# One expert-weight unit per branch, nine raw buffers, and a reordered start, in a two-layer hybrid trunk

## Chip, cores and metric

One core of one Trainium2 chip runs the whole program. The metric is device time in microseconds (us), the median of three runs. Engine names are those of the profile: PE (matrix products), DVE, ACT, POOL (element-wise work), SP (here it only issues loads).

## What is computed

A two-layer trunk on 256 tokens of 1024 columns, all in float32. Each layer has a token mixer and a feed-forward part; each part is normed, modulated by a vector that is computed from `c`, and added to the residual. Layer 0 has a dense SwiGLU, layer 1 a mixture of eight experts, of which each token takes two. The lines that matter here:

```python
c_act = jax.nn.silu(c)                                   # c: (1, 1024)
for l in range(2):
    mod = (c_act @ ada_w[l] + ada_b[l])[:, None, :]      # ada_w[l]: (1024, 6144)
    sh1, sc1, gt1, sh2, sc2, gt2 = jnp.split(mod, 6, axis=-1)
    h = rms_norm(x, norm_mix[l]) * (1.0 + sc1) + sh1
    x = x + gt1 * hybrid_mixer(h, ...)
    h = rms_norm(x, norm_ffn[l]) * (1.0 + sc2) + sh2
    f = swiglu(h, ...) if l == 0 else moe_swiglu(h, router_w, router_b, w1, w3, w2)
    x = x + gt2 * f
return rms_norm(x, final_norm)
# moe_swiglu: logits = h @ router_w + router_b; the two largest, softmax over them; per expert e, over its tokens:
#   y = (silu(xb @ w1[e]) * (xb @ w3[e])) @ w2[e]        # w1, w3: (1024, 3584), w2: (3584, 1024)
```

## The kernel before

The program runs in four phases: mixer 0, dense layer 0, mixer 1, experts (from about 1000 us to the end). A float32 product is made of faster ones: a weight tile `raw` is cast to `hl` by ACT, and the remainder `raw - hl` goes to `lo` on DVE; a product then takes three matmuls, hi by hi, hi by lo and lo by hi.

**The start.** `ada_first` (L232) issues eight loads of 1 MB of `ada_w` on SP's queue into a ring of seven buffers `f`, and between them, by `load_rows` (L156), the first columns of the constants `cst` and `x`. `c` is loaded on ACT's queue as a column `csil` (L145), each of its 1024 numbers a piece of its own. `setup(l)` (L170) loads five small tables of layer `l` on ACT's queue into a tile `rows`. `Router.__init__` (L1111) loads the router's bias and weights there too. The scheduler may issue a load that waits for nothing long before its place in the code; so the tables of layer 1 and of the router are issued at the start of the program. Eight semaphores, DMAHW0 to DMAHW7, are given to the transfers of all queues in turn; a load waits where it would take one whose earlier transfer it must see done.

**The experts.** `experts` (L1285) goes through eight experts. `w1`, `w3` and `w2` of one are cut in 42 units of 1 MB ([128, 2048]). For each unit `Weights.load` (L1255, issue at L324 on SP) fetches it into one of seven raw buffers, and `Weights.unit` makes two casts on ACT (L1267) and one subtraction on DVE (L1271), whichever arm will use it. `split(4)` keeps up to four units so split (rings `hl` and `lo` of four). PE takes two units at a time: `group` (L1278) hands them out, and `Light.arms` (L1218) puts a branch around them, on a register that holds whether the expert has at most 64 tokens:

```python
for u0 in range(0, KC // kc, 2):
    units = weights.group()
    light.arms(e, lambda: few(u0, units), lambda: heavy(u0, units))
    weights.after = None
    weights.load(5)
```

`few` multiplies `raw` directly in float32 (L1372, L1454), `heavy` the split parts (L1351, L1438, L1443), 24 matmuls of 512 columns for two units of `up`. `up` makes the hidden values, block by block of 1024 columns or 512; `turned` (L1405) transposes and splits them, with side work on ACT and DVE (L1416, L1417, L1519); `down` multiplies them by `w2`. With this input experts 0, 2, 4 and 6 are heavy, 1, 3, 5 and 7 light, so heavy and light stages alternate. The program has both arms of every branch, and `order` rows below show both.

`route` (L1154) finds each token's two experts and their places, builds the flags (`Light`, L1196; eight loads into PE's registers at L1207), and then the mixing weights. `gather` (L1290) collects the tokens of a pair of experts by matmuls with 0/1 matrices `pe` (L1314). `begin(e)` (L1389) makes the transposed matrix `pte` and the weight column `ws` with which `finish` (L1465) writes the expert's result back.

Of the kernel before, what the change touches and what calls it, by code (L numbers as in the profile page):

```python
# [19 lines left out]
P = 128  # L20
# [10 lines left out]
NE = 8  # L31
# [42 lines left out]
def trunk_kernel(  # L74
# [17 lines left out]
    phase_b = dict(raw2=4, hl2=1, lo=4, r4=6, x32=3, s32=1, t2=5, t2r=6, gt=1, xn=2, pe=2, pte=2)  # L92
# [3 lines left out]
        hl2=[P, 2048], lo=[P, 2048],  # L96
# [73 lines left out]
    def setup(l):  # L170

        rows = pc.tile([P, 2, P], F32, tag="rows", name=f"rows{l}")
        G.memset(rows, 0.0)
        nc.scalar.dma_start(rows[0:48, 0, :], ada_b[l].rearrange("(r p) -> r p", p=P))
        nc.scalar.dma_start(rows[48:56, 0, :], norm_mix[l].rearrange("(r p) -> r p", p=P))
        nc.scalar.dma_start(rows[56:64, 0, :], norm_ffn[l].rearrange("(r p) -> r p", p=P))
        nc.scalar.dma_start(rows[64:65, 0, :], dn_out_norm[l : l + 1, :])
        nc.scalar.dma_start(rows[0:96, 1, :], conv_w[l].rearrange("j (r p) -> (j r) p", p=P))
# [53 lines left out]
    def ada_first(l, mods):  # L232

        cs = mk("r4", [P, 4 * S])[:, : 32 * KC].rearrange("p (k c) -> p k c", c=32)
        V.tensor_copy(cs, csil.unsqueeze(2).broadcast_to([P, KC, 32]))
        banks = {m: [bank(t) for _ in range(2)] for m, t in zip(mods, "gs")}
        raws = {}
        for m in mods:
            for q in range(4):
# [3 lines left out]
                if len(raws) == 5:  # L243
                    rest = setup(0)
        for m in mods:
# [912 lines left out]
    def route():  # L1158
# [21 lines left out]
        wgt = sm([P, 2, 2])  # L1180
        V.tensor_sub(wgt, m8[:, :, 0:2], m8[:, :, 0:1].broadcast_to([P, 2, 2]))
        A.activation(wgt, wgt, AF.Exp)
        den = sm([P, 2])
        V.tensor_reduce(den, wgt, AX.X, ALU.add)
        V.reciprocal(den, den)
        V.tensor_tensor(wgt, wgt, den.unsqueeze(2).broadcast_to([P, 2, 2]), ALU.mult)
        V.tensor_tensor(wt, eq, wgt[:, :, 0:1].broadcast_to([P, 2, NE]), ALU.mult)
        V.tensor_tensor(tmp, tmp, wgt[:, :, 1:2].broadcast_to([P, 2, NE]), ALU.mult)
        V.tensor_add(wt, wt, tmp)
        return oa, wt, pos, light  # L1190

    zero = pc.tile([P, P], F32R, tag="zero", name="zero")
    most = pc.tile([P, 1], F32, tag="most", name="most")
    mosti = pc.tile([P, 1], I32, tag="mosti", name="mosti")

    class Light:  # L1196


        def __init__(self, cnt):
# [4 lines left out]
            self.back = pc.tile([P, NE], F32, tag="back", name="back")  # L1204
            V.tensor_scalar(self.back, self.flag, -float(P // 2), None, ALU.mult)
            self.regs = [
                nc.values_load(self.int[0:1, e : e + 1], engines=[mybir.EngineType.PE], min_val=0, max_val=1)  # L1207
                for e in range(NE)
            ]

        def slots(self, e):

            t = mk("t2", [P, 512])[:, 0:P]
            V.tensor_scalar(t, C["iota"], P // 2 - 0.5, self.back[:, e : e + 1], ALU.is_gt, ALU.mult)
            V.tensor_add(t, t, C["iota"])
            return t

# [6 lines left out]
    class Weights:  # L1224
# [53 lines left out]
        def group(self):  # L1278

            self.load(2)  # L1280
            self.split(4)
            return [self.ready.popleft() for _ in range(2)]

    def experts(l, weights, xnh, xnl, oa, wt, pos, light, merge):
# [50 lines left out]
        def up(e, n):  # L1335
# [8 lines left out]
            def heavy(u0, units):  # L1344
                for u, (_, hv, lv) in enumerate(units):
                    for w, xs in ((hv, (xh, xl)), (lv, (xh,))):
                        for k in range(kc):
                            kk = kc * (u0 + u) + k
                            for x_ in xs:
                                for b, ps in enumerate(banks):  # L1350
                                    T.matmul(  # L1351
                                        ps, x_[:, kk, :], w[:, k, 512 * b : 512 * b + 512],
                                        start=(kk == 0 and x_ is xh and w is hv), stop=(kk == KC - 1 and w is lv),
                                    )
# [9 lines left out]
            def few(u0, units):  # L1364
                wide = len(banks) > 1
                if u0 == 0 and not wide:
                    blank()
                for u, (w, _, _) in enumerate(units):
                    for k in range(kc):
                        kk = kc * (u0 + u) + k  # L1370
                        for i, h in enumerate(halves):
                            T.matmul(  # L1372
# [299 lines left out]
```

## Time and profile before

| | us |
|---|---|
| median of three runs | 1970.7 |
| the three runs | 1968.8, 1970.7, 1971.07 |
| time of the profiled execution | 1972.13 |
| span of its trace | 1970.3 |

The profile is of one execution. Its page gives the busy time of each engine over the whole span, which mixes phases with different limits; views of a stretch (busy time in a window, waits in a window, the chain of waits that ended last) tell what bounds that stretch. "Granted clock" is the share of PE's full clock that the chip allowed. A row such as `x32 7.09` is a run of 32 like instructions that took 7.09 us together; what stands in brackets behind it is the idle time before, and what ended it. Names ending in q (SPq, ACTq, PEq) are the issuing side of an engine.

### The profile page before, as it was taken

The page shows a single profiled execution, that of the slowest core. Times are in us where ns is not written, and L with a number is a line of the kernel's source. Part 1 is how long each engine was busy: PE and PEld are TensorE (multiplying, and loading weights), DVE is VectorE, ACT ScalarE, POOL GpSimd, SP SyncE. Part 2 cuts the span into 40 slices and gives each one's busy share as a digit, 9 for nine tenths or more (in the row PEclk, how much of TensorE's full clock was granted, in tenths as well). Part 3 has the DMA queues.
Part 4 walks back from the last instruction along what each step waited for, and adds up shares of the span by engine and source line. Part 5 has one row for each costly group of instructions (what it writes and reads, how often), then busy time and mean ns, then how long its engine had stood idle before and what let it go on. Part 6 is the DMA issues. An engine that isn't in the chain of part 4 may idle for free.

```text
span 1970.3 us, 36475 instructions
## 1 busy us (share of the span) xinstructions
PE 1823.6 (93%) x14868; PEld 1412.8 (72%) x14868; DVE 1599.0 (81%) x1900; ACT 1283.3 (65%) x1842; POOL 80.0 (4%) x88
## 2 busy tenths in 40 slices
PE   5899999999999899999979988999889998899986
PEld 2889989999999789989968733686337863378522
DVE  3778678687666878588668898997989889898998
ACT  2765556454443665556477788877788687886885
POOL 0101000000000101000000002000020001000000
PEclk8999999999999999999989999999899998899998
DMA  8544447688773344555739999999999999999995
GB/s 279 168 155 144 143 153 235 214 288 279 246 260 95 127 153 131 162 171 193 259 140 377 365 402 348 380 369 365 381 355 383 367 370 365 370 374 368 377 403 232
DMA packets 220334, 539.24 MB, mean 274 GB/s; under 512 B 13602, under 2 KB 120548, under 8 KB 206052
## 3 DMA queue, kind: packets, MB, share of 16 engines
q1 hardware_dynamic: 215216, 536.02, 74.7%
q8 instruction: 148, 2.42, 0.5%
q10 hardware_dynamic: 4916, 0.35, 0.2%
q14 instruction: 54, 0.44, 0.1%
HBM read 535.27 MB, written 1.06 MB: 272 GB/s over the span
## 4 chain that ended last, share of the span: by engine, by line
PE 63%; DVE 18%; ACT 8%; issue 7%; DMA 4%; DVEq 0%; SPq 0%; ACTq 0%
PE g L1351 15%; PE g L379 7%; PE g L375 7%; PE g L377 7%; DVE lo L1271 7%; PE a L1438 4%; PE g L1372 3%; ACT hl L1267 3%; DMA raw<-in_moe_w_dram 2%; PE a L1454 2%; PE a L1443 2%; DVE t L627 2%; DVE hl L340 2%; ACT hl L339 1%; PE a L1055 1%
## 5 line engine op out<-in xcount | busy, mean ns | idle before, releaser
L1271 DVE TENSOR_TENSOR lo<-raw,hl 128x2048 fp32r<-128x2048 f32 (+1 forms) x338 | 754.1, 2272 | 46.5 <-ACT hl L1267 46.4
L1267 ACT CAST hl<-raw 128x1024 fp32r<-128x1024 f32 x672 | 657.3, 1052 | 26.0 <-DMA raw<-in_moe_w_dram 21.6
L340 DVE TENSOR_TENSOR hl<-raw,hl 128x1024 fp32r<-128x1024 f32 (+1 forms) x252 | 298.1, 1188 | 136.8 <-ACT hl L339 136.4
L339 ACT CAST hl<-raw 128x1024 fp32r<-128x1024 f32 (+1 forms) x252 | 256.8, 1022 | 201.3 <-PE g L379 134.0
L375 PE MATMUL g<-r,hl 128*128 128x256 f32 x1536 | 235.2, 293 | 6.6 <-ACT r L483 3.4
L377 PE MATMUL g<-r,hl 128*128 128x256 f32 x1536 | 228.6, 288 | 0.0
L379 PE MATMUL g<-r,hl 128*128 128x256 f32 x1536 | 223.9, 287 | 0.4 <-DVE hl L340 0.4
L1351 PE MATMUL g<-hl,r 128*128 128x512 f32 x896 | 222.9, 391 | 0.0
L375 PEld LDWEIGHTS g<-r,hl 128*128 128x128 f32 x1536 | 204.2, 194 | 15.2 <-ACT r L483 4.7
L1372 PE MATMUL g<-raw,x 128*64 128x512 f32 (+1 forms) x1024 | 212.1, 563 | 0.0
L377 PEld LDWEIGHTS g<-r,hl 128*128 128x128 f32 x1536 | 204.6, 195 | 3.0 <-issue 2.5
L379 PEld LDWEIGHTS g<-r,hl 128*128 128x128 f32 x1536 | 202.6, 194 | 2.6 <-issue 1.9
L1351 PEld LDWEIGHTS g<-hl,r 128*128 128x128 f32 x896 | 167.4, 188 | 37.0 <-ACT hl L1267 2.4
L1372 PEld LDWEIGHTS g<-raw,x 128*64 128x64 f32 x1024 | 71.5, 141 | 114.6 <-issue 104.2
L1454 PE MATMUL a<-raw,s 128*64 128x512 f32 x448 | 120.2, 684 | 3.6 <-ACT s L1420 3.2
L1351 PE MATMUL g<-lo,r 128*128 128x512 f32 x448 | 120.7, 391 | 0.5
L1416 ACT CAST t2r<-a 128x512 fp32r<-128x512 f32 x56 | 32.8, 585 | 113.1 <-PE a L1412 113.1
L1351 PEld LDWEIGHTS g<-lo,r 128*128 128x128 f32 x448 | 83.6, 188 | 20.0 <-DVE lo L1271 2.9
L210 DVE SCALAR_TENSOR_TENSOR f<-raw,csil,f 128x1024 f32<-128x1024 f32 x70 | 92.5, 1322 | 5.7 <-DMA raw<-in_ada_w_dram 5.2
L1438 PE MATMUL a<-hl,t2r 128*128 128x512 f32 x224 | 89.0, 397 | 1.7 <-ACT hl L1267 1.7
L1454 PEld LDWEIGHTS a<-raw,s 128*64 128x64 f32 x448 | 34.3, 157 | 74.5 <-issue 67.3
L1443 PE MATMUL a<-hl,t2r 128*128 128x512 f32 x224 | 87.5, 390 | 0.0
(334 smaller groups left out, 2211.6 us busy)
## 6 DMA issues: line engine op xcount, KB each, us to landing
raw<-in_moe_w_dram SPq DMA_DIRECT2D x334, 1024.0 KB, 7.0
raw<-in_w_in_dram SPq DMA_DIRECT2D x60, 1024.0 KB, 5.4
raw<-in_ffn_w_dram SPq DMA_DIRECT2D x42, 1024.0 KB, 5.8
raw<-in_ada_w_dram SPq DMA_DIRECT2D x40, 1024.0 KB, 5.3
f<-in_ada_w_dram SPq DMA_DIRECT2D x8, 1024.0 KB, 8.6
raw<-in_w_up_dn_dram SPq DMA_DIRECT2D x8, 1024.0 KB, 5.1
raw<-in_w_out_dram SPq DMA_DIRECT2D x8, 1024.0 KB, 5.0
raw<-in_w_up_sb_dram SPq DMA_DIRECT2D x4, 1024.0 KB, 5.1
```

Source lines behind the costliest of these rows:

```text
L339: A.copy(hv, part)
L340: V.tensor_sub(lv, part, hv.bitcast(F32))
L375: T.matmul(pv[:, b, :], hv[:, k, :], xh[:, k, :], start=(k == 0), stop=False)
L377: T.matmul(pv[:, b, :], hv[:, k, :], xl[:, k, :], start=False, stop=False)
L379: T.matmul(pv[:, b, :], lv[:, k, :], xh[:, k, :], start=False, stop=(k == kc - 1))
L1267: A.copy(hi[:, h, :], raw[:, h, :])
L1271: V.tensor_sub(lo[:, h, :], raw[:, h, :], hi[:, h, :].bitcast(F32))
L1351: T.matmul(ps, x_[:, kk, :], w[:, k, 512 * b : 512 * b + 512], start=(kk == 0 and x_ is xh and w is hv), stop=(kk == KC - 1 and w is lv),)
L1372: T.matmul(banks[0][h, 0:half], x32[:, kk, :], w[:, k, half * i : half * i + half], start=(wide and kk == 0), stop=(kk == KC - 1), skip_gr ...
L1438: T.matmul(ye[nb], gh[:, gs], w[:, k, nw], start=(first and q == 0 and u == 0 and p == 0), stop=(last and u == 1 and p == 3),)
L1443: T.matmul(ye[nb], gl[:, gs], w[:, k, nw], start=False, stop=False)
L1454: T.matmul(ye[nb][h, :], g32[:, gs], w[:, k, 512 * nb : 512 * nb + 512], start=False, stop=(last and u == 1 and k == 1), skip_group_check= ...
```

## The change

* **Start.** `c` is loaded as eight rows (`crow`), goes through Silu as rows, and is transposed on PE and copied to `csil` on DVE. The first columns of `cst` are the first load of SP. `setup(0)` is called after the fourth `ada_w` load instead of the fifth. The loads of `setup(1)` and of the router keep their place in the code.
* **Units.** `take` hands out one unit, and a branch stands around each. Nine raw buffers for seven (`raw2` 6 for 4, three as before in the other ring), three `hl` and three `lo` for four; `load(6)` for `load(5)`, `split(3)` for `split(4)`, `load(9)` for `load(5)` before the phase. `s32` has two buffers for one, `pte` one for two.
* **Flags and slots.** The register load of an expert's flag moves to `fetch(e)`, called by `begin(e)`. What else `begin` did is now `slots(e)`, called before the expert's last `down`; `Light.slots` is one operation for two, with a constant `foldr` made once by POOL. The mixing weights (`mix`) are made after the first gather.

The diff, cut:

```diff
@@ -89,11 +89,11 @@
-    phase_b = dict(raw2=4, hl2=1, lo=4, r4=6, x32=3, s32=1, t2=5, t2r=6, gt=1, xn=2, pe=2, pte=2)
+    phase_b = dict(raw2=6, lo=3, r4=6, x32=3, s32=2, t2=5, t2r=6, gt=1, xn=2, pe=2, pte=1)
...
+        lo=[P, 2048],
     )
@@ -142,10 +142,12 @@
 
 
     csil = pc.tile([P, KC], F32, tag="csil", name="csil")
-    nc.scalar.dma_start(csil, c_in[0].rearrange("(k p) -> p k", p=P))
-    A.activation(csil, csil, AF.Silu)
+    crow = pc.tile([KC, P], F32, tag="crow", name="crow")
+    nc.scalar.dma_start(crow, c_in[0].rearrange("(k p) -> k p", p=P))
+    A.activation(crow, crow, AF.Silu)
     cst = pc.tile([P, _CST.shape[1]], F32, tag="cst", name="cst")
     first = CST["i32"][1]
+    nc.sync.dma_start(cst[:, :first], cst_in[:, :first])
...
 
     def load_rows():
-        nc.sync.dma_start(cst[:, :first], cst_in[:, :first])
         nc.sync.dma_start(x, x_in[0].rearrange("(b p) d -> p b d", p=P))
@@ -169,13 +170,14 @@
 
     def setup(l):
 
-        rows = pc.tile([P, 2, P], F32, tag="rows", name=f"rows{l}")
+        pin = tc.keep_in_program_order if l else lambda ins: ins
+        rows = mk("t2", [P, 512])[:, 0 : 2 * P].rearrange("p (i c) -> p i c", c=P)
         G.memset(rows, 0.0)
-        nc.scalar.dma_start(rows[0:48, 0, :], ada_b[l].rearrange("(r p) -> r p", p=P))
-        nc.scalar.dma_start(rows[48:56, 0, :], norm_mix[l].rearrange("(r p) -> r p", p=P))
-        nc.scalar.dma_start(rows[56:64, 0, :], norm_ffn[l].rearrange("(r p) -> r p", p=P))
-        nc.scalar.dma_start(rows[64:65, 0, :], dn_out_norm[l : l + 1, :])
...
+        pin(nc.scalar.dma_start(rows[64:65, 0, :], dn_out_norm[l : l + 1, :]))
@@ -232,7 +234,6 @@
     def ada_first(l, mods):
 
         cs = mk("r4", [P, 4 * S])[:, : 32 * KC].rearrange("p (k c) -> p k c", c=32)
-        V.tensor_copy(cs, csil.unsqueeze(2).broadcast_to([P, KC, 32]))
         banks = {m: [bank(t) for _ in range(2)] for m, t in zip(mods, "gs")}
         raws = {}
         for m in mods:
@@ -240,8 +241,12 @@
                 raws[m, q] = ada_load(l, m, q, "f8")
                 if len(raws) == 2:
                     load_rows()
-                if len(raws) == 5:
+                if len(raws) == 4:
                     rest = setup(0)
+        ps = bank("a")
+        T.transpose(ps[:, 0:KC], crow, ident[0:KC, 0:KC])
+        V.tensor_copy(csil, ps[:, 0:KC])
+        V.tensor_copy(cs, csil.unsqueeze(2).broadcast_to([P, KC, 32]))
         for m in mods:
             for q in range(4):
                 rv = raws[m, q]
...
         def __init__(self, l, j):
-            nc.scalar.dma_start(rb, router_b[j : j + 1, :].partition_broadcast(P))
-            nc.scalar.dma_start(rw[:, 0], router_w[j].rearrange("(k p) n -> p k n", p=P))
+            tc.keep_in_program_order(nc.scalar.dma_start(rb, router_b[j : j + 1, :].partition_broadcast(P)))
@@ -1201,19 +1210,18 @@
             V.tensor_copy(self.int, self.flag)
-            self.back = pc.tile([P, NE], F32, tag="back", name="back")
-            V.tensor_scalar(self.back, self.flag, -float(P // 2), None, ALU.mult)
-            self.regs = [
-                nc.values_load(self.int[0:1, e : e + 1], engines=[mybir.EngineType.PE], min_val=0, max_val=1)
-                for e in range(NE)
-            ]
+            self.regs = {}
 
         def slots(self, e):
 
             t = mk("t2", [P, 512])[:, 0:P]
-            V.tensor_scalar(t, C["iota"], P // 2 - 0.5, self.back[:, e : e + 1], ALU.is_gt, ALU.mult)
-            V.tensor_add(t, t, C["iota"])
+            V.scalar_tensor_tensor(t, foldr, self.flag[:, e : e + 1], C["iota"], ALU.mult, ALU.add)
             return t
+
+        def fetch(self, e):
+            self.regs[e] = nc.values_load(
+                self.int[0:1, e : e + 1], engines=[mybir.EngineType.PE], min_val=0, max_val=1
+            )
 
@@ -1275,11 +1283,11 @@
             while len(self.ready) < n and self.loaded:
                 self.ready.append(self.unit(*self.loaded.popleft()))
 
-        def group(self):
-
-            self.load(2)
-            self.split(4)
-            return [self.ready.popleft() for _ in range(2)]
+        def take(self):
+
+            self.load(1)
+            self.split(3)
...
-            for u0 in range(0, KC // kc, 2):
-                units = weights.group()
-                light.arms(e, lambda: few(u0, units), lambda: heavy(u0, units))
+            for u in range(KC // kc):
+                unit = weights.take()
+                light.arms(e, lambda: few(u, *unit), lambda: heavy(u, *unit))
                 weights.after = None
-                weights.load(5)
+                weights.load(6)
                 yield
             yield banks
 
         st = {}
 
         def begin(e):
+            light.fetch(e)
+            st[e] = []
+
+        def slots(e):
 
             ps = bank("a")
             for b in range(2):
@@ -1400,7 +1410,7 @@
             A.copy(pte, ps[:, 0:S])
             ws = sm([P, 1])
             V.tensor_copy(ws, ps[:, S : S + 1])
-            st[e] = (pte, ws, [])
+            return pte, ws
 
...
@@ -1521,16 +1529,19 @@
 
         gath = {}
         drain([gather(0)])
+        merge.begin()
         late = None
         for e in range(NE):
             begin(e)
             for f, n in blocks:
                 ss, g = hidden(e, n, late)
                 if late:
+                    if late[1:3] == blocks[-1]:
+                        ends = slots(late[0])
                     for _ in down(*late[:3], *g):
                         step()
                     if late[1:3] == blocks[-1]:
-                        steps.append(finish(late[0]))
+                        steps.append(finish(late[0], *ends))
                         step()
                 late = (e, f, n, ss)
@@ -1542,17 +1553,19 @@
         while steps:
             step()
         g = turned(late[3])
+        ends = slots(late[0])
         drain([down(*late[:3], *g)])
         merge.end()
-        finish_last(late[0])
+        finish_last(late[0], *ends)
...
+        G.tensor_scalar(foldr, C["iota"], P // 2 - 0.5, -float(P // 2), ALU.is_gt, ALU.mult)
         with tc.high_priority(offset=0):
-            weights.load(5)
+            weights.load(9)
             weights.split(2)
-        oa, wt, pos, light = route()
+        oa, wt, pos, light, mix = route()
...
             gt = None
+            mixed = False
+
+            def begin(self):
+                if not self.mixed:
+                    self.mixed = True
+                    mix()
```

The loads on SP's queue, from the program's start to the first weight of the mixer. `f_6` to `f_14` are the pieces of `ada_w`, `x` the tokens; what stands behind "waits" names the semaphore of an earlier transfer (the transfers of all queues take DMAHW0 to DMAHW7 in turn) or an engine. Before:

```order
L198 DMA f_6_100<-in_ada_w_dram 128x2x1024
L198 DMA f_7_102<-in_ada_w_dram 128x2x1024
L157 DMA cst<-in_cst_dram 128x160 [waits DMAHW3_49]
L158 DMA x<-in_x_dram 128x2x1024 [waits DMAHW4_49]
L198 DMA f_8_106<-in_ada_w_dram 128x2x1024 [waits DMAHW6_49]
L198 DMA f_9_108<-in_ada_w_dram 128x2x1024 [waits DMAHW2_49]
L198 DMA f_10_110<-in_ada_w_dram 128x2x1024 [waits DMAHW4_49]
L198 DMA f_11_119<-in_ada_w_dram 128x2x1024 [waits DMAHW5_49]
L198 DMA f_12_121<-in_ada_w_dram 128x2x1024 [waits DMAHW6_49]
L198 DMA f_13_123<-in_ada_w_dram 128x2x1024 [waits DMAHW7_49,DMAHW1_49,PE_49]
```

There every load behind `f_7` waits for an earlier transfer, among them those of ACT's queue. With the change:

```order
L150 DMA cst<-in_cst_dram 128x160
L200 DMA f_6_102<-in_ada_w_dram 128x2x1024
L200 DMA f_7_104<-in_ada_w_dram 128x2x1024
L159 DMA x<-in_x_dram 128x2x1024 [waits DMAHW2_49]
L200 DMA f_8_107<-in_ada_w_dram 128x2x1024 [waits DMAHW3_49]
L200 DMA f_9_109<-in_ada_w_dram 128x2x1024 [waits DMAHW4_49]
L200 DMA f_11_118<-in_ada_w_dram 128x2x1024 [waits DMAHW5_49]
L200 DMA f_12_120<-in_ada_w_dram 128x2x1024 [waits DMAHW6_49]
L200 DMA f_13_122<-in_ada_w_dram 128x2x1024 [waits DMAHW7_49]
L200 DMA f_14_124<-in_ada_w_dram 128x2x1024 [waits DMAHW0_49,PE_49]
```

`cst` is now first and waits for nothing; counted in the order of issue, the waits of the second listing fall on `ada_b` (DMAHW2), `f_6` (3), the norm rows (4, 5), `dn_out_norm` (6), `f_7` (7) and `conv_w` (0), and the last of them on PE.

PE's queue between the router and the first expert: `lighti` are the flags, `pe` and `xn` the operands of the gather. Before, the last three of the eight flag loads and the gather's first rows:

```order
L1207 TENSOR_LOAD lighti
L1207 ISA x2
L1207 TENSOR_LOAD lighti
L1207 ISA x2
L1207 TENSOR_LOAD lighti
L1207 ISA x2
L1314 MATMUL a_12313<-pe_12296,xn_12288 128x256 [waits DVE_49,PE_49,Activation_49]
L1314 MATMUL a_12313<-pe_12296,xn_12289 128x256
L1314 MATMUL a_12313<-pe_12296,xn_12288 128x256 [waits DVE_49,Activation_49]
```

All eight loads stand ahead of the gather. With the change, from the router's last matmul to the gather's first rows:

```order
L1181 MATMUL a_12200<-rt,ones 128x8 x2
L1222 TENSOR_LOAD lighti [waits DVE_49]
L1222 ISA x2
L1222 TENSOR_LOAD lighti
L1222 ISA x2
L1322 MATMUL a_12232<-pe_12217,xn_12209 128x256 [waits DVE_49,PE_49,Activation_49]
L1322 MATMUL a_12232<-pe_12217,xn_12210 128x256
L1322 MATMUL a_12232<-pe_12217,xn_12209 128x256 [waits DVE_49,Activation_49]
```

Two loads are left ahead of the gather. Behind the gather's 32 matmuls, from the seventh load to the heavy arm of the first unit:

```order
L1222 TENSOR_LOAD lighti
L1222 ISA x2
L1222 TENSOR_LOAD lighti
L1222 ISA x2
L1227 COMPARE_AND_BRANCH
L1378 MATMUL g_12324<-raw_1354_12157,x_1379_12226 64x512 [waits DMAHW6_49,Pool_49]
L1378 MATMUL g_12324<-raw_1354_12157,x_1379_12226 64x512 x3
L1366 MATMUL g_12325<-r_1381_12228,zero 128x512 [waits Activation_49]
L1227 UNCONDITIONAL_BRANCH
L1358 MATMUL g_12324<-hl_12175,r_1381_12228 128x512 [waits Activation_49]
```

The other six loads stand between the gather and the first branch. A branch stands around each unit: `raw` is read by the light arm, `hl` and then `lo` by the heavy one, with 12 matmuls.

## Rows read from the trace of the kernel before

**Rows 1.** Page, engines' busy time over the span.

```profile
PE 1823.6 (93%) x14868; PEld 1412.8 (72%) x14868; DVE 1599.0 (81%) x1900; ACT 1283.3 (65%) x1842; POOL 80.0 (4%) x88
```

**Rows 2.** Chain of waits, 0 to 70 us: start, length, what.

```profile
11.28 8.80 DMA rw<-in_router_w_dram
...
22.37 13.17 DMA f<-in_ada_w_dram
35.59 1.94 PE s L252 x8
```

**Rows 3.** Waits of SP's queue, 0 to 40 us: total, times, longest.

```profile
SPq L198 <- DMA rw<-in_router_w_dram: 8.6, 1, 8.6
SPq L157 <- DMA rows<-in_norm_mix_dram: 8.4, 1, 8.4
```

**Rows 4.** Transfers, 0 to 40 us, GB/s in each microsecond.

```profile
GB/s 0 41 193 332 340 223 361 398 245 3 38 142 221 410 317 133 318 421 320 94 0 135 360 369 385 434 385 393 410 426 418 418 422 410 372 360 349 380 400 156
```

**Rows 5.** Windows: PE, PEld, DVE, ACT, POOL busy; clock, DMA share, GB/s.

```profile
22.00:36.00 14.00, 10.91 (x62) 3.53 (x60) 3.36 (x9) 0.00 (x0) 0.41 (x2) 0.92 1.01 397
1244.00:1364.00 120.00, 119.57 (x539) 95.70 (x536) 107.44 (x67) 91.94 (x106) 0.00 (x0) 1.00 0.98 370
1364.00:1483.00 119.00, 102.20 (x464) 42.47 (x462) 111.06 (x81) 96.65 (x122) 10.17 (x8) 0.91 0.97 370
1842.00:1952.00 110.00, 94.66 (x434) 37.11 (x434) 108.93 (x68) 92.09 (x107) 0.00 (x0) 0.95 0.96 380
```

**Rows 6.** Waits of DVE, 1364 to 1483 us: total, times, longest.

```profile
DVE lo L1271 <- ACT hl L1267: 7.3, 6, 2.3
```

**Rows 7.** Timeline of DVE, 1364 to 1485 us: start, length, what.

```profile
1378.30 8.90 DVE L1271 TENSOR_TENSOR lo<-raw,hl 128x2048 fp32r<-128x2048 f32 x4 [1.45 <-ACT hl L1267]
...
1465.82 11.14 DVE L1271 TENSOR_TENSOR lo<-raw,hl 128x2048 fp32r<-128x2048 f32 x5 [1.73 <-ACT hl L1267]
```

**Rows 8.** Timeline of ACT, 1364 to 1485 us.

```profile
1375.30 1.05 ACT L1267 CAST hl<-raw 128x1024 fp32r<-128x1024 f32 x1 [2.11 <-DMA raw<-in_moe_w_dram]
...
1463.53 0.37 ACT L1400 CAST pte<-a 128x256 fp32r<-128x256 f32 x1 [2.43 <-PE a L1398]
```

**Rows 9.** Timeline of ACT's queue, 0 to 13 us.

```profile
1.30 0.58 ACTq L174 DMA_DIRECT2D rows<-in_ada_b_dram  x1
```

**Rows 10.** Tile lighti: durations in ns (min, median, max), first and last start.

```profile
L1207 PEldq TENSOR_LOAD <-lighti x8: 297/302/492, 1000.9 to 1005.9; - x8
```

**Rows 11.** Timeline of PE, 1000 to 1014 us.

```profile
1006.72 5.76 PE L1314 MATMUL a<-pe,xn 128*128 128x256 f32 x32 [6.51 <-issue]
```

**Rows 12.** Chain of waits, 1000 to 1045 us.

```profile
1013.10 27.23 PE g L1351 x120
```

**Rows 13.** Line 1219, the branches: durations in ns.

```profile
L1219 PEldq COMPARE_BRANCH  x252: 65/179/413, 1010.9 to 1950.7; - x126
```

**Rows 14.** Timeline of PE, 1364 to 1400 us, light arms.

```profile
1368.83 7.09 PE L1372 MATMUL g<-raw,x 128*64 128x512 f32 x32
```

**Rows 15.** Groups of instructions, whole span: busy, mean ns, idle before, releaser.

```profile
L1271 DVE TENSOR_TENSOR lo<-raw,hl 128x2048 fp32r<-128x2048 f32 (+1 forms) x338 | 754.1, 2272 | 46.5 <-ACT hl L1267 46.4
L1267 ACT CAST hl<-raw 128x1024 fp32r<-128x1024 f32 x672 | 657.3, 1052 | 26.0 <-DMA raw<-in_moe_w_dram 21.6 <-DVE lo L1271 2.5 <-PE g L1351 0.9
...
L1417 DVE TENSOR_TENSOR t2r<-a,t2r 128x512 fp32r<-128x512 f32 x56 | 38.3, 684 | 24.3 <-ACT t2r L1416 24.3
...
L1519 DVE TENSOR_TENSOR t<-t,g 128x512 f32<-128x512 f32 x56 | 36.1, 680 | 1.0 <-PE g L1351 1.0
...
L1416 ACT CAST t2r<-a 128x512 fp32r<-128x512 f32 x56 | 32.8, 585 | 113.1 <-PE a L1412 113.1
```

**Rows 16.** Page, transfers: count, size, us to landing.

```profile
out_dram<-raw SPq DMA_DIRECT2D x4, 256.0 KB, 2.0
```

More of the change, by code (lines that the diff above doesn't have):

```diff
@@ L1342, in up, with heavy @@
             kc, half = 2048 // n, n // 2
[L1344 to L1354, printed above, removed]
+            def heavy(u, _, hv, lv):
+                for w, xs in ((hv, (xh, xl)), (lv, (xh,))):
+                    for k in range(kc):
+                        kk = kc * u + k
+                        for x_ in xs:
+                            for b, ps in enumerate(banks):
+                                T.matmul(
+                                    ps, x_[:, kk, :], w[:, k, 512 * b : 512 * b + 512],
+                                    start=(kk == 0 and x_ is xh and w is hv), stop=(kk == KC - 1 and w is lv),
+                                )
             def blank():
@@ L1426, in down @@
             first, last = f == 0, f + n == DFF
-            ye = st[e][2]
+            ye = st[e]
             if first:
                 ye.extend(bank("a") for _ in range(2))
-            def heavy(q, units):
-                gh, gl = parts[q]
-                for u, (_, hv, lv) in enumerate(units):
-                    for p, (k, w) in enumerate(((0, hv), (1, hv), (0, lv), (1, lv))):
-                        gs = slice((2 * u + k) * P, (2 * u + k + 1) * P)
-                        for nb in range(2):
-                            nw = slice(512 * nb, 512 * nb + 512)
-                            T.matmul(
-                                ye[nb], gh[:, gs], w[:, k, nw], start=(first and q == 0 and u == 0 and p == 0),
-                                stop=(last and u == 1 and p == 3),
-                            )
-                            if p < 2:
-                                T.matmul(ye[nb], gl[:, gs], w[:, k, nw], start=False, stop=False)
@@ L1445, in few, with heavy @@
-            def few(q, units):
-                if first and q == 0:
+            def heavy(m, _, hv, lv):
+                (gh, gl), u = parts[m // 2], m % 2
+                for p, (k, w) in enumerate(((0, hv), (1, hv), (0, lv), (1, lv))):
+                    gs = slice((2 * u + k) * P, (2 * u + k + 1) * P)
+                    for nb in range(2):
+                        nw = slice(512 * nb, 512 * nb + 512)
+                        T.matmul(
+                            ye[nb], gh[:, gs], w[:, k, nw], start=(first and m == 0 and p == 0),
+                            stop=(last and m == n // 256 - 1 and p == 3),
+                        )
+                        if p < 2:
+                            T.matmul(ye[nb], gl[:, gs], w[:, k, nw], start=False, stop=False)
@@ L1447, in few @@
+            def few(m, w, *_):
+                if first and m == 0:
                     for nb in range(2):
                         T.matmul(ye[nb], zero, parts[0][0], start=True, stop=True, skip_group_check=True)
-                for u, (w, _, _) in enumerate(units):
-                    i, at = (q, u) if n > 512 else (u, 0)
-                    for k in range(2):
-                        gs = slice((2 * at + k) * P + i * HS, (2 * at + k) * P + i * HS + HS)
-                        for nb, h in enumerate(halves):
-                            T.matmul(
-                                ye[nb][h, :], g32[:, gs], w[:, k, 512 * nb : 512 * nb + 512],
-                                start=False, stop=(last and u == 1 and k == 1), skip_group_check=True,
-                            )
@@ L1459, in down @@
-            for q in range(n // 512):
-                units = weights.group()
-                light.arms(e, lambda: few(q, units), lambda: heavy(q, units))
-                weights.load(5)
+                i, at = divmod(m, n // 512)
+                for k in range(2):
+                    gs = slice((2 * at + k) * P + i * HS, (2 * at + k) * P + i * HS + HS)
+                    for nb, h in enumerate(halves):
+                        T.matmul(
+                            ye[nb][h, :], g32[:, gs], w[:, k, 512 * nb : 512 * nb + 512],
+                            start=False, stop=(last and m == n // 256 - 1 and k == 1), skip_group_check=True,
+                        )
@@ L1463, in down, with finish @@
+            for m in range(n // 256):
+                unit = weights.take()
+                light.arms(e, lambda: few(m, *unit), lambda: heavy(m, *unit))
+                weights.load(6)
                 yield
-        def finish(e):
-            pte, ws, ye = st.pop(e)
+        def finish(e, pte, ws):
+            ye = st.pop(e)
             ys = [mk("t2", [P, 512]) for _ in range(2)]
```

60 lines of the change are left out of this document (32 added, 28 removed).

## The prediction

> **What bounds the kernel now.** I read the page first. PE is busy 93% of the span [rows 1], but that is a mean over phases, so I went on to the phases that the diff touches: the program's first 40 us, and the expert phase, which runs from about 1000 us to the end.
>
> *The start* is bound by a queue that runs dry. The chain of waits there is almost all transfer: 8.80 us for the router's table, then 13.17 us for the last piece of `ada_w`, then PE at 35.59 [rows 2]. SP's own waits say what it stood for: 8.4 us for a norm row of 4 KB, 8.6 us for the router's table [rows 3]. Neither is data that SP or the next matmul needs. The listing of the order shows why: each SP load waits for the semaphore of an earlier transfer, whichever queue that came from. While SP stands, nothing is left to move: 3 GB/s in the tenth microsecond, 0 in the 21st [rows 4]; from 22 us on, with nothing in its way, the stream runs at 397 [rows 5].
>
> *The expert phase* is an alternation. In a heavy expert's stage (1244 to 1364 us) PE is busy 119.57 of 120 us at a granted clock of 1.00 (2.4 GHz): nothing but fewer matmuls shortens it. In a light expert's (1364 to 1483) PE has 102.20 of 119, and DVE 111.06: DVE, which splits every unit whether or not the arm taken reads the split, ends last there [rows 5]. The 8 us between 119 and 111 are DVE's idle time, and 7.3 us of them are waits for ACT's casts [rows 6]. Two of DVE's waits have their cause one step further back: 1.45 us at 1378, where ACT itself had waited 2.11 us for a raw unit, and 1.73 us at 1465, where ACT had waited 2.43 us for PE to finish the transposes of `begin` before it could copy `pte` [rows 7, 8].
>
> **Part by part.** The sum is made against the profiled execution's own 1972.13 us.
>
> *First loads.* After the change the tables of layer 1 and the router no longer stand in the start's queues, `c` comes as 8 rows instead of 1024 pieces of four bytes, and `cst` goes first. By the listing, the second group of loads waits for `ada_b`, `f_6`, the two norm rows, `dn_out_norm`, `f_7`, all issued before it, and only the eighth `ada_w` load also waits for PE (a ring of seven). PE can begin on `f_6` once `crow` and `cst` are in and one transpose and two copies are through. So I let the queue never run dry. What must land before the last matmul of this stage is eight units and `x` of 1024 KB each and 80 KB of constants, 9.52 MB. At the 397 of the undisturbed stretch [rows 5] that is 24.0 us; the first bytes move at 2 us [rows 4], so it lands at 26.4, not at the 35.54 where the last piece's transfer ends [rows 2]: **−9.1 us**. Bounds: the best microsecond of that row (434) gives 23.9 and −11.6; the 340 of the fifth, the best while the stream still starts up, gives 30.0 and −5.5. I take 397 because it holds for 14 us on end. PE needs 1.94 us behind the last unit now [rows 2] and will again.
>
> *Moved loads.* Seven issues on ACT's queue, each at most 0.58 us [rows 9], now stand in the dense layer and the second mixer, where ACT casts ahead of PE. Taken at 0, covered by the casts already made (three or four units, by the listing); without that cover 7 × 0.58 = +4.1.
>
> *Flags.* Today eight register loads stand on PE's queue before the gather, from 1000.9 to 1005.9 us, 0.72 us apart, and the gather's 32 matmuls begin at 1006.72 after 6.51 us of standing [rows 10, 11]. After the change two stand before them; the other six follow the gather and are still ahead of the first branch, so "expert by expert" is not what the listing shows. Two loads end near 1002.3, the 32 matmuls (5.76) at 1008.1, six loads (4.3) at 1012.4; the first up matmuls, which stand at 1013.10 now [rows 12], can follow the branch near 1012.6: **−0.5**. If the loads run ahead of the matmuls still under way, it is at best 0.5 + 4.3 = 4.8; at worst 0, as `mix` only moves.
>
> *One unit per branch.* 168 branches become 336, and half of the added ones (84) lie in heavy stages, where PE has no room. The branch itself reads 0.179 us in the median and 0.413 at most [rows 13]. But today's branches cost nothing that shows: 120 matmuls of a heavy arm, five groups with their jumps between them, take 27.23 us, 0.227 each [rows 12], and 32 of a light arm, two groups, 7.09 us, 0.222 each [rows 14]. Taken at 0. If each stood in the open: 84 × 0.179 = 15 us, or 34 at the longest; nothing points there.
>
> *Nine raw buffers for seven, three split buffers for four.* Two more units are under way when a stage turns. In heavy stages this buys nothing (PE). In a light stage it removes the late raw unit behind the 1.45 us. With it goes the 1.73: `slots` stands just before the expert's last `down`, one block into the next stage, no longer where an expert begins, so ACT need not stand on `pte` between two casts at the turn. I take both, 3.2 us, in the three light stages that have a stage before and behind: 3 × 3.2 = **−9.5** (rounded). Bounds: 0, if DVE's idle time reappears elsewhere in the stage; and 3 × (119 − 111) = −24, DVE with no idle left. The last light stage has DVE at 108.93 of 110 [rows 5]: nothing to take. The three split buffers are weighed below, with the two units prefetched at the start of the phase, which only feed a heavy stage: 0.
>
> *One vector operation for two in each `slots`, a larger `s32`, one `pte`*: under 1 us each way, 0.
>
> **Sum**: 1972.13 − 9.1 − 0.5 − 9.5 = 1953.0. The profiled execution lies 1.4 us above the median of the runs, so **1952**.
>
> One rule speaks against this change. The heavy row has no room for a stall at a jump: 0.227 us a matmul through five groups, jumps and all [rows 12]. The Trainium skill (Runtime: NRT & Kernel Launch, Instruction fetch mechanics) says that a taken branch whose target is outside the current window breaks the sequential prefetch, so that the engine stalls on a fetch by DMA; the change doubles such jumps. The trace disagrees for jumps over 24 or 32 matmuls, and the change makes them shorter.
>
> **The rivals.**
>
> *Only the start pays.* Light stages may be bound by the stream: 42 units of 1024 KB are 44.0 MB, at the 370 of that stage 119 us, exactly its length, with the DMA engines 0.97 busy. Then more buffers only wait longer. Against: heavy stages show the same 0.98 while units wait for PE, so a full queue reads as busy there; and the last light stage moved 380, the start 397 [rows 5]. It gives 1952 + 9.5 = 1961.
>
> *All of DVE's idle time in the light stages goes*, −24 in place of −9.5: 1937. For: nine units deep, every late unit is covered. Against: part of the idle time is ACT's, 96.65 busy of 119, whose casts DVE must follow [rows 5].
>
> *Slower: three split buffers bind the heavy stages.* A unit's buffers come free when its arm ends. The split of the unit three on then needs two casts (2 × 1.05) and a subtraction (2.27), 4.3 us [rows 15]. Until PE reads that `lo`, two arms pass (24 matmuls, 5.45) and the `hl` part of the third (8 matmuls, 1.81): 7.26, so 3.0 to spare. Into that fall a block's side operations, two or three each of 0.585, 0.684 and 0.680: 4.5 us if they come together [rows 15]. It decides from 3.0 on: 1.5 us a block, 14 blocks of 1024 columns in the heavy experts, 20 us, and the light gain is gone with it: 1961 + 20 = 1981. Against: side operations are spread over two engines and many units, and a pair-wise ring of four has the same 3.0 for its first unit, with PE at 119.57 of 120.
>
> *The start does not pay* (a wait on PE or on `crow` replaces those removed): 1952 + 9.1 = 1961 too. *Nothing pays*: 1972 less the 1.4, 1971.
>
> *Every added jump stalls.* The shortest transfer of the page lands in 2.0 us [rows 16]; 168 × 2.0 = 336, so 2288. This is the time by the page named above.
>
> **How the numbers follow.** Forecast (1944 to 1960) 0.53; only the start pays 0.19; all idle time gone 0.12; the start does not pay 0.04; three buffers bind, 1981, 0.08; nothing, 1971, 0.03; jumps stall 0.01. The range runs from 1936, just past the case of 1937, to 1967, the case of 1961 with a start at its weak bound (+3.6) and a margin of 2: it leaves out the slower cases, the 1971 and the far ends, under 0.2. About 0.2% (3.9 us) is what a measurement of this kernel can tell from no change, so "same" is 1966.8 to 1974.6: the case of 1971 and the weak ends of the two at 1961, 0.06. Slower: 0.08 and 0.01, less the part of it that stays within: 0.08. Faster: the rest, 0.86.
>
> **What would show it.** In the changed profile: SP's waits in the first 40 us no longer name `norm_mix` or the router's table, no microsecond between 3 and 26 is near 0 GB/s, and the `s` matmuls of the last `ada_w` piece end near 28 instead of 37.5 us. Light stages of some 116 us, heavy ones still 120 with PE over 0.99. Wrong would be: heavy stages with PE waiting for `lo` or `hl` (then three buffers), light stages of 119 with ACT waiting for `raw` (then the stream), or PE gaps of more than 0.2 us before the first matmul of each arm (then the branches).

## The result

The change is slower: a median of 1994.0 us (four runs, 1986.6 to 2004.0) against 1970.9, ratio 1.0123 with a 95% interval of 1.0077 to 1.0168. The profiled execution took 1995.24 us, its span is 1993.5. 1952 was forecast, in a range that ended at 1967.

**The start** came out as forecast in its transfers and not in its time. Transfers of the change, 0 to 40 us, GB/s in each microsecond:

```profile
GB/s 0 35 141 300 359 369 394 409 316 306 411 407 407 398 415 411 406 402 406 406 414 406 414 406 414 410 406 362 353 351 398 319 297 343 360 338 354 310 80 9
```

No hole is left from 3 to 37 us (in [rows 4] the stream fell to 3 and 0). But the first matmuls of the mixer, at 42.00 us in the trace before, stand at 39.60: 2.4 us are won, not 9.1. The timeline of PE before:

```profile
42.00 1.83 PE L503 MATMUL a<-r,hl 128*128 128x256 f32 x7 [3.43 <-DVE t L484]
```

The timeline of ACT, and under it that of PE, in the changed kernel:

```profile
20.46 0.30 ACT L499 CAST hl<-t 128x128 fp32r<-128x128 f32 x1 [16.11 <-DMA t<-in_w_in_dram]
...
20.91 0.64 ACT L416 ACTIVATE t<-x 128x512 f32<-128x512 f32 x1
```

```profile
30.84 3.66 PE L257 MATMUL s<-f,r 128*32 128x512 f32 x32
...
39.60 1.83 PE L508 MATMUL a<-r,hl 128*128 128x256 f32 x7 [3.44 <-DVE t L489]
```

ACT stood 16.11 us on a small table, the narrow weights (64 KB), that had been issued at 3.18 us and came in beside the full stream. Behind that cast wait the squares of `x` (L416), then the norm on DVE, its transposes on PE, and behind those on PE's queue the `s` matmuls. These ran 32 in a row without a wait for a load: their `ada_w` pieces were there already.

How long that table takes differs from execution to execution. Eight of the kernels below have the same start; in their traces its cast stands between 10.20 us (e8) and 20.33 (e9), and the mixer's first matmuls stand with it between 34.54 and 39.77. In the three where the cast comes before 13 us (e3, e7, e8) the mixer begins at 34.5 to 34.9. So the wait explains the missing time, but it is not there each time.

**The flags**: loaded from 996.2 us, first up matmul at 1005.48, a stretch of 9.3 us; before it was 1000.9 [rows 10] to 1012.86, 12.0. Here the change won 2.7 us. The flag loads and the first up matmuls of the change, and below them the first up matmuls before:

```profile
L1222 PEldq TENSOR_LOAD <-lighti x8: 295/304/491, 996.2 to 1004.5; - x8
...
1005.48 0.74 PE L1358 MATMUL g<-hl,r 128*128 128x512 f32 x2 [0.99 <-ACT t L1333]
```

```profile
1012.86 1.39 PE L1351 MATMUL g<-hl,r 128*128 128x512 f32 x5
```

**The expert phase** lost all of that and more. By the first up matmuls of all experts, the three light stages that are followed by another are together 12.6 us longer than before, and the four heavy ones 13.2. Windows of the change, columns as in [rows 5]; the bounds are the first up matmuls of successive experts, a heavy, a light and a heavy stage:

```profile
1241.30:1366.00 124.70, 121.59 (x536) 95.36 (x534) 107.49 (x66) 93.59 (x107) 0.00 (x0) 0.99 0.94 352
1366.00:1491.90 125.90, 105.46 (x465) 44.48 (x464) 112.14 (x80) 98.54 (x123) 4.03 (x8) 0.89 0.94 358
1491.90:1615.60 123.70, 121.36 (x537) 95.47 (x535) 106.59 (x66) 91.93 (x106) 0.00 (x0) 0.99 0.94 350
```

These heavy stages are 4 us longer than the 120 of [rows 5], the light one, which lost most of the three, 7 longer than its 119, and DVE's work there is about the same (112.14 against 111.06): what grew is idle time. The groups of the cast and of the subtraction over the whole span, as in [rows 15]:

```profile
L1275 ACT CAST hl<-raw 128x1024 fp32r<-128x1024 f32 x672 | 659.8, 1049 | 83.9 <-PE g L1358 38.6 <-PE g L1378 19.2 <-PE a L1452 11.6
...
L1279 DVE TENSOR_TENSOR lo<-raw,hl 128x2048 fp32r<-128x2048 f32 (+1 forms) x338 | 754.4, 2273 | 83.4 <-ACT hl L1275 82.3
```

Casts stood idle 26.0 us before, 21.6 of them for raw units; now 83.9, of which 38.6, 19.2 and 11.6 for PE. The subtractions wait 82.3 us for casts (46.4 before). By the program, what a cast can wait for on PE is a free `hl` buffer. The timeline of ACT in the second heavy stage, of the change:

```profile
1249.36 2.00 ACT L1275 CAST hl<-raw 128x1024 fp32r<-128x1024 f32 x2 [0.91 <-PE g L1358]
1252.08 2.00 ACT L1275 CAST hl<-raw 128x1024 fp32r<-128x1024 f32 x2 [0.72 <-PE g L1358]
1254.80 1.05 ACT L1275 CAST hl<-raw 128x1024 fp32r<-128x1024 f32 x1 [0.72 <-PE g L1358]
1258.49 1.09 ACT L1523 ACTIVATE t<-g 128x512 f32<-128x512 f32 x2 [2.63 <-PE g L1358]
1259.46 12.43 ACT L1275 CAST hl<-raw 128x1024 fp32r<-128x1024 f32 x13
```

and of the kernel before, at the same place:

```profile
1247.96 6.76 ACT L1267 CAST hl<-raw 128x1024 fp32r<-128x1024 f32 x7
1255.93 1.09 ACT L1515 ACTIVATE t<-g 128x512 f32<-128x512 f32 x2 [1.22 <-PE g L1351]
1256.90 4.85 ACT L1267 CAST hl<-raw 128x1024 fp32r<-128x1024 f32 x5
```

Before, seven casts ran on end. With three buffers they go in step with PE: 2.00 us of casting and 0.72 of standing make 2.72, one heavy arm. ACT, which has 0.72 us to spare in each unit, cannot use it to get ahead. Then the Silu of the block (L1523) comes up in ACT's queue, waits 2.63 us for PE to finish the bank, and the next casts stand behind it. DVE, with nothing cast ahead, stands too (timeline of DVE, the change, the same place):

```profile
1260.55 8.90 DVE L1279 TENSOR_TENSOR lo<-raw,hl 128x2048 fp32r<-128x2048 f32 x4 [4.13 <-ACT hl L1275]
```

Before, the idle time of DVE that ended the same way there, at 1257.99 us, was 0.56 us.

### The profile page after: what moved, and what is told of

It reads as the page before. It is cut to its first block, busy times and chain, and to the rows that moved or that the text cites. A ratio compares the mean times of both kernels' runs of the same rounds, so it can differ in the third digit from the quotient of the medians.

```text
span 1993.5 us, 36782 instructions
## 1 busy us (share of the span) xinstructions
PE 1827.2 (92%) x14869; PEld 1413.0 (71%) x14869; DVE 1598.8 (80%) x1892; ACT 1291.4 (65%) x1842; POOL 65.9 (3%) x89
## 5 line engine op out<-in xcount | busy, mean ns | idle before, releaser
L1279 DVE TENSOR_TENSOR lo<-raw,hl 128x2048 fp32r<-128x2048 f32 (+1 forms) x338 | 754.4, 2273 | 83.4 <-ACT hl L1275 82.3
L1275 ACT CAST hl<-raw 128x1024 fp32r<-128x1024 f32 x672 | 659.8, 1049 | 83.9 <-PE g L1358 38.6
L1358 PE MATMUL g<-hl,r 128*128 128x512 f32 x896 | 229.4, 399 | 1.7 <-ACT t L1333 1.0
L1378 PE MATMUL g<-raw,x 128*64 128x512 f32 (+1 forms) x1024 | 205.4, 544 | 0.0
L1358 PEld LDWEIGHTS g<-lo,r 128*128 128x128 f32 x448 | 84.2, 189 | 23.3 <-DVE lo L1279 5.9
L632 DVE SCALAR_TENSOR_TENSOR t<-t,conv,t 128x255 f32<-128x255 f32 (+2 forms) x144 | 61.8, 476 | 26.3 <-ACT t L627 26.2
L1422 PE MATMUL a<-cst,t 128*128 128x128 f32 x224 | 40.2, 319 | 45.4 <-DVE t L1527 45.4
```

Source lines behind the costliest of these rows:

```text
L1275: A.copy(hi[:, h, :], raw[:, h, :])
L1279: V.tensor_sub(lo[:, h, :], raw[:, h, :], hi[:, h, :].bitcast(F32))
L1358: T.matmul(ps, x_[:, kk, :], w[:, k, 512 * b : 512 * b + 512], start=(kk == 0 and x_ is xh and w is hv), stop=(kk == KC - 1 and w is lv),)
L1378: T.matmul(banks[0][h, 0:half], x32[:, kk, :], w[:, k, half * i : half * i + half], start=(wide and kk == 0), stop=(kk == KC - 1), skip_gr ...
```

## The experiments

Ten kernels, compared with the kernel before on the same chip: e1 to e4 on one, e6 to e12 on another, so between these two groups the ratios are the better measure. "Stages" are the third heavy and third light ones in each, by the first up matmuls. The kernel before has 120.3 and 118.6 there, the change 123.7 and 120.7.

| | edit | median us | ratio to before [95%] | stages |
|---|---|---|---|---|
| e1 | before + start | 1967.2 | 0.9981 [0.9969, 0.9994] | 120.5, 118.2 |
| e2 | change, four split, seven raw | 1956.5 | 0.9923 [0.9902, 0.9944] | 121.2, 114.1 |
| e3 | change, seven raw | 1994.7 | 1.0118 [1.0101, 1.0136] | 123.7, 120.7 |
| e4 | e2 with two units per branch | 1953.9 | 0.9908 [0.9894, 0.9922] | 119.2, 114.1 |
| e6 | e4, narrow cast late | 1950.9 | 0.9913 [0.9898, 0.9928] | 119.2, 112.8 |
| e7 | change, four `hl`, three `lo`, eight raw | 1960.0 | 0.9960 [0.9945, 0.9975] | 121.5, 114.0 |
| e8 | change, five split, five raw | 2024.1 | 1.0279 [1.0255, 1.0302] | 125.1, 124.0 |
| e9 | e4, slots at `begin`, two `pte`, one `s32` | 1963.6 | 0.9973 [0.9963, 0.9984] | 121.9, 113.9 |
| e10 | e4, one `s32` | 1954.0 | 0.9920 [0.9906, 0.9934] | 120.4, 115.1 |
| e12 | e2, narrow cast late | 1956.0 | 0.9929 [0.9915, 0.9943] | 121.2, 114.4 |

**The split ring: e2, e3, e7, e8.** e2's edit:

```diff
-    phase_b = dict(raw2=6, lo=3, ...)
+    phase_b = dict(raw2=4, hl2=1, lo=4, ...)
-            self.split(3)
+            self.split(4)
-                weights.load(6)
+                weights.load(4)
```

> The change with four hl and four lo buffers and seven raw ones (split(4)), one unit per branch as in the change. If three split buffers are the cause, the loss goes and the start's gain stays: 1960 to 1967. If one branch per unit is the cause, or the moved slots, it stays near 1994.

e3 has e2's raw ring (`raw2=4`, `load(4)`) and the change's split ring:

> The change with seven raw buffers in place of nine, still three hl and three lo. If the two added raw buffers were worth anything in the light stages, it is slower than the change by up to 10 us (2004); if the split ring binds, raw units only wait longer and it is the same, 1994.

e2 and e3 differ in the split ring alone, and lie 38.2 us apart; e3 and the change differ in the raw ring alone, and lie 0.7 us apart, well inside their spread. So three split buffers are the whole loss, and the two added raw buffers were worth nothing beside them; nine raw buffers beside four split ones were not run. e2, at 1956.5, came out below both of its expected values: something behind the start gains as well (e9 and e10 below). The windows of the second heavy and second light stage, of e3:

```profile
1241.80:1364.00 122.20, 119.82 (x536) 94.24 (x534) 106.50 (x66) 92.04 (x105) 0.00 (x0) 1.00 0.97 359
1364.00:1490.90 126.90, 107.25 (x466) 44.84 (x465) 112.25 (x80) 98.84 (x123) 4.04 (x8) 0.88 0.95 351
```

and of e2:

```profile
1239.00:1360.00 121.00, 119.36 (x538) 96.02 (x538) 110.74 (x68) 95.72 (x110) 0.00 (x0) 1.00 1.00 380
1360.00:1473.50 113.50, 98.96 (x462) 41.11 (x461) 107.67 (x78) 93.36 (x118) 6.75 (x8) 0.94 0.97 374
```

The light stage loses most, 13.4 us against 1.2 in the heavy one of this pair. This is the largest pair: over the whole phase the three light stages differ by 31.7 us together, the four heavy ones by 4.9 and the last light one by 2.6.

The counts of DVE's operations say where a part of the 13.4 comes from. With four buffers DVE does two operations more in the heavy stage (68 for 66, 4.2 us) and two fewer in the light one (78 for 80, 4.6 us): they are subtractions, 45 and 41 of them with four buffers, 43 and 43 with three. So a heavy stage, where DVE has time left, makes two units more for the light stage behind it. The rest is idle time of DVE in the light stage, 5.8 us with four buffers and 14.7 with three; its waits for casts there are 5.7 and 10.5 us.

e7 takes the two split rings apart:

```diff
+            while len(self.ready) < n + 1 and self.loaded:
+                self.ready.append(self.cast(*self.loaded.popleft()))
+            for u in list(self.ready)[:n]:
+                if u[2] is None:
+                    self.rest(u)
```

`cast` fills `hl`, for one unit more than `rest`, which fills `lo`; rings of four `hl`, three `lo`, eight raw.

> The change with four hl buffers, three lo buffers and eight raw ones: casts run one unit further ahead, subtractions as in the change. In the trace of the change ACT waits 38.6 us on PE for an hl buffer and DVE 82.3 us on ACT. If the cast's buffer is the link that binds, most of the loss goes: 1957 to 1965. If the subtraction's buffer binds as much, it stays at 1985 to 1994.

1960.0: with one more `hl` buffer it is within 3.4 us of e2 by the medians, 7 by the ratios. The link that binds most is the cast's buffer, not the subtraction's; whether what is left belongs to the `lo` ring is not shown, since the raw ring and the order of the operations differ from e2 as well. Its cast and subtraction groups, and the subtractions of e2:

```profile
L1284 DVE TENSOR_TENSOR lo<-raw,hl 128x2048 fp32r<-128x2048 f32 (+1 forms) x338 | 752.5, 2273 | 31.3 <-ACT hl L1274 26.7 <-issue 3.8
L1274 ACT CAST hl<-raw 128x1024 fp32r<-128x1024 f32 x672 | 655.6, 1054 | 53.2 <-PE g L1366 31.7 <-issue 11.4 <-DMA raw<-in_moe_w_dram 6.3
...
L1279 DVE TENSOR_TENSOR lo<-raw,hl 128x2048 fp32r<-128x2048 f32 (+1 forms) x338 | 755.9, 2275 | 65.6 <-ACT hl L1275 64.6
```

DVE's waits for casts over the whole span fall from 82.3 to 26.7 us. That sum is no measure of the time, though: e2 has 64.6 of them and is the faster kernel. ACT still stands 31.7 us on PE in e7: so that wait alone is not the loss either. e8 goes on in the same direction with five of each (`raw2=2, hl2=2, lo=5`, `split(5)`, `load(1)`):

> The change with five hl, five lo and five raw buffers. If the depth of the split ring is a wait that four buffers cover, it equals e2: 1956. If depth still pays at four, light stages fall further, below 114 us: 1945 to 1953. If five raw buffers let the stream run dry, ACT waits for raw units and it is slower than e2: above 1962.

2024.1: with only five raw buffers both kinds of stage run at 124 to 125 us, and over the whole span casts wait 157.0 us for raw units, as its third case has it (23.3 in e2). What a fifth split buffer is worth by itself stays open, since it could only be had from the raw ring.

**The start: e1, e6.** e1 is the kernel before with the edits of the start and the pinned loads, none of the expert phase.

> The kernel before with the reordered start and the pinned loads alone; the expert phase as before. In the trace of the change the router's flags are loaded 4.7 us earlier than before (996.2 against 1000.9), so the start should be worth about that: 1966 us. If the start gave nothing that lasts, 1971; if its whole predicted gain lasted, 1962.

0.19% faster, 1.2 to 6.1 us, 2.8 by the medians: what is left of the predicted 9.1. In its trace the mixer begins at 37.10 us, 4.9 earlier than before; where the other 2 us go was not followed up. e6 takes the suspected stand away, on top of e4:

```diff
         wraw = narrow_load(wsrc, 16)
         ...
+        with tc.issue_after(late.ins) if late else nullcontext():
+            A.copy(wv[:, :, 0:n], raw)
```

`late` is the last of the squares of `x`.

> The kernel of e4 with one more edit: at the start, ACT casts the narrow weights after the squares of x instead of ahead of them. In the trace of the change ACT stands 16.1 us on that small load (cast at 20.46) while x is there, and the norm, the transposes and the second half of the first modulation queue behind it. If that stand is what took the start's gain, the first mixer matmul moves from 39.6 to about 33.6 us and the time falls 6 us below e4: 1948. If the stream of large loads binds the start, nothing moves: 1954.

Timeline of PE, e6:

```profile
28.82 1.91 PE L257 MATMUL s<-f,r 128*32 128x512 f32 x8 [0.67 <-DMA f<-in_ada_w_dram]
...
35.23 1.36 PE L514 MATMUL a<-r,hl 128*128 128x256 f32 x7 [3.44 <-DVE t L489]
```

The `s` matmuls wait for `ada_w` again, and the mixer begins at 35.23, 6.8 us earlier than in the trace before and 3.7 earlier than e4's 38.92. 33.6 was expected; the three kernels whose table landed early begin at 34.5 to 34.9 without the edit. But in e6 the table landed late, its cast stands at 20.52, and the mixer did not wait for it: that the edit takes the wait away is shown in the trace. Its time is 3.0 us below e4 by the medians, while the ratios of the two (taken on different chips) do not tell them apart.

**Pairs, slots, `s32`: e4, e9, e10, e12.** e4 is e2 with `group` and pair-wise branches as before:

> The change with two units per branch, seven raw, four hl and four lo buffers as before, so that of the expert phase only flags, slots, mixing weights, s32 and pte are changed. If split buffers or branches are the cause, 1960 to 1967; if the later slots or the single pte buffer are, it stays above 1985.

1953.9, below both cases: neither the later slots nor the single `pte` buffer makes the loss, and part of the rest is a gain.

e9 puts the transposes and the `pte` copy back:

```diff
         def begin(e):
             light.fetch(e)
             st[e] = []
+            early[e] = slots(e)
```

> The kernel of e4 with the transposes and the pte copy back at the expert's begin, with two pte buffers and one s32 buffer as before. If the moved slots (or the second s32) shorten the light stages of e4 from 118 to 113 to 117 us, they go back to 118 and the time rises by 8 to 13 us: 1962 to 1967. If the flags and mixing weights made the gain, it stays at 1954.

e10 is e4 with `s32=1`:

> The kernel of e4 with one s32 buffer as before; the slots stay late and pte single. Between e9 (slots early, one s32: 1963.6) and e4 (slots late, two s32: 1953.9) it says which of the two edits is worth the 9.7 us. If the late slots are, 1954; if the second s32 is, 1963.

e10 equals e4, so the second `s32` buffer gives nothing; e9, which differs from e10 in the place of the slots and the second `pte`, is 9.5 us slower. By the medians the late slots, with the single `pte`, are worth that. In e9's profile, however, not each light stage went back to 118 (they are 118.3, 115.6 and 113.9 us, against 116.5, 113.5 and 115.1 in e10, and three heavy stages are 1.1 to 1.5 longer). From the first up matmul of the first expert to that of the last, the two profiles differ by 7.0 us, 2.7 in the light stages and 4.2 in the heavy ones. The first up matmul itself stands 4.3 us later in e9; 3.0 of these lie ahead of the gather, where the two programs do the same. So 7 to 9.5.

> The kernel of e2 (one unit per branch, four split buffers, seven raw) with the late narrow cast of e6. It is e6 but for 168 more branches. If a branch costs nothing that shows, it equals e6, 1951; by the worst reading of a branch in heavy stages (84 times 0.179 us) it would be 1966.

One unit per branch against two: e2 against e4 +2.6 us, e12 against e6 +5.1, each near the edge of its intervals. Handing out one unit for each branch costs something between nothing and 5 us; how much of it is the branch itself is not shown. The third heavy stage shows it (121.2 against 119.2), and that is far from 15 us, let alone from a stall of 2 us at each jump.

**The sum** by medians: start −2.8, flags and mixing weights −3.6 (e9 against e1), late slots −9.5, `s32` 0, one unit per branch +2.6, split ring +38.2, raw ring −0.7: +24.2, against the measured +23 to +24. The kernels form a chain from before to the change (e1, e9, e10, e4, e2, e3), so the steps have to add up to the whole and their sum confirms nothing; each step stands on its own pair. Those of the flags and of `s32` cross the two chips, and by the ratios neither e1 and e9 nor e10 and e4 are told apart. e6 has the lowest median, but by the ratios it and e4 (0.9913 and 0.9908) are equal: 0.9% below the kernel before.

## Why the prediction was wrong

* **What bounds, and the rows:** right as far as they went. DVE ends last in light stages, PE bounds the heavy ones, and the start stood on a dry queue; that a second wait stood behind it did not show in the chain of the kernel before.
* **First loads, −9.1:** mis-sized; e1 measured −2.8. The stream never ran dry. A small part is arithmetic: 2 us and 24.0 make 26.0, not 26.4, so by its own terms the sum was −9.5; and in e6, where PE waits for the last piece again, it begins on it at 28.82. The step that failed is the list of "what must land before the last matmul of this stage": it leaves out the narrow weights, and so takes the last piece of `ada_w` for the last event. Behind the wait removed stood another on ACT, a 64 KB load that landed before 13.6 us in the trace before and at 20.4 in that of the change. With it out of the way (e6) the mixer begins 6.8 us early. The rival "the start does not pay" had it that a wait replaces those removed, but on PE or on `crow`.
* **Flags, −0.5:** the mechanism was right, and the loads ran beside the matmuls, as the better bound had it; 2.7 us in the trace.
* **One unit per branch, 0:** near enough, 0 to 5 us. A stall at each jump does not show: 168 more jumps do not cost 336 us. Whether any of them leaves the window that the rule weighed there speaks of, no run here shows, so these runs do not speak against the rule itself.
* **Nine raw, −1.45 in each light stage:** nothing seen (e3 against the change). The late raw unit was real, but casts that wait for a split buffer do not need a unit sooner.
* **Late slots, −1.73 in each light stage:** the gain is there and larger than the 5.2 of three stages, 7 to 9.5 us in all, but not where the forecast had it: by the profiles of e9 and e10 2.7 us of it lie in the light stages and 4.2 in the heavy ones, which were to gain nothing. Why heavy stages gain stays open.
* **Three split buffers, taken at no cost:** this is the step that failed and turned the sign: a term of 0, where e3 against e2 measured +38.2. The rival named the ring, counted a spare time of 3.0 us for a unit and 4.5 us of side work that would have to fall into it, and priced the heavy stages at 20 us and the light ones at their lost gain. It was then given 0.08, because "side operations are spread over two engines and many units, and a pair-wise ring of four has the same 3.0". Both are beside the point. The spare time was counted for one unit in a steady run; what the ring holds is the lead that covers a stop of an engine whose queue is in order. ACT's Silu waits 2.63 us for PE with the casts behind it, and with three buffers the lead is a unit shorter and cannot be built up again, since each cast waits for its arm. And a light stage was only charged with a lost gain, but the three of them took 31.7 us of the loss: with a unit of lead less, less of their work was done in the heavy stage ahead, and DVE, which ends last there, stood longer. The heavy stages, priced at 20, took 4.9.

The two rivals at 1961 and the one at 1937 did not come about. The slower one named the right ring and the right sign; that its 1981 lies near 1994 is in part luck, since it put the loss in the wrong stages. So is it that e2, the change with four split buffers, measured 1956.5 beside the forecast of 1952: the start gave a third of its term, the slots more than theirs.

## What to carry to other kernels

In this kernel a ring between engines whose queues keep their order was worth its lead, not its throughput. Count how long the producer's queue can be held by an instruction that waits for the consumer, and ask whether the units already made cover that. Taking a buffer from the ring that is full to give it to one upstream moves the lead to where it can't be used: look at which ring's waits show in the trace (here raw units, 4.0 us in a light stage) and how close the other one is to showing. When a wait is removed from a start, follow the in-order queues for the next late transfer before booking the whole wait.

## What was not expected of the hardware

A small load of 64 KB took 17.2 us from issue to landing beside the full stream of large loads in the trace of the change, where at the start of the kernel before, with holes in the stream, the same load, issued at 10.16, had landed by 13.6. In the eight kernels with the same start, issued at the same 3.18 us beside a stream as full, it took between 6.9 us (e8) and 17.1 (e9). What decides between the two was not found.

The time ahead of the expert phase varies with it. The first up matmul stood between 1001.6 and 1008.8 us in profiles of kernels whose program up to there is the same but for the number of weight units fetched ahead; the three traces where the small load landed early (e3, e7, e8) have it at 1001.6 to 1003.2, the others at 1004.4 or later. So a single trace does not tell a gain of 4 us there.
